# A linear layer with a low-rank update: all loads ahead of all stores, with transposed x kept on chip in bf16

## The chip, the cores and the metric

The kernel runs on one core of a Trainium2 chip. The metric is the device time of one execution in microseconds (us). The median of three runs of the kernel before is 165.0 us (164.87 to 165.51).

## The reference

`x` is 16 x 2048 rows of 256 numbers in float32, taken as 32,768 rows. `W` is 256 x 256, the low-rank part has rank 16.

```python
x_flat = x.reshape(-1, in_dim)
y = x_flat @ W
lora_out = x_flat @ lora_A
lora_out = lora_out * lora_E
lora_out = lora_out @ lora_B
y = y + scale * lora_out
```

The kernel folds the low-rank part into the weights once (`weff` = W + scale x A diag(E) B, in bf16) and then computes x times `weff`.

## The kernel before

Rows are spread over 128 partitions; a "row" below is one row of 256 numbers in each partition (128 KB over all partitions), so x has 256 such rows. `PLAN` cuts them into eight chunks of 16 to 48 rows. x arrives in float32 in the ring `xy` of 176 rows, and y is written over the same places, from which it is stored. So chunks 6 and 7 can be loaded only when stores have freed their places.

Per group of 16 rows (`G`), and in it per step of 8 rows (`S`):

- DVE casts 16 rows from `xy` to `xb` in bf16 (L199).
- PE transposes 8 rows at a time into PSUM (`ps_xt`, two buffers, L222); pairs of bf16 numbers travel as one float32, so a row takes one transpose of 128 columns.
- DVE copies the transposes of a step from PSUM into one of two buffers `xt` (L213).
- PE multiplies: for each half step of 4 rows (`Q`), 8 matmuls with `xt` as the loaded weights and `weff` moving, into one of two PSUM buffers `ps_y` (L230). Ahead of each half it waits for the buffer to be free (L227).
- ACT copies the half from `ps_y` into `xy` (L177); the last six halves are copied by DVE. The last copy of a chunk raises `s_rdy`, on which SP waits for the store; POOL hands the signal on to `s_y`, on which PE waits.

PE's work stands in one loop of 16 turns (L249), in which every address is fixed. The other engines' instructions are written out. All DMAs are issued by SP, in this order: W, chunk 0, the three small low-rank inputs, chunks 1 to 5, stores 0 to 2, loads 6 and 7, stores 3 to 7. So loads come first, then three stores, then two loads, then five stores. Three transfers are cut in two (`TAIL`), and stores 0 and 3 wait until the head of the load ahead of them has landed. `PAUSE` makes DVE wait ahead of chunk 4 until store 2 has landed.

Of the kernel before, what the change touches and what calls it, by code (L numbers as in the profile page):

```python
# [6 lines left out]

PLAN = [16, 32, 48, 48, 16, 16, 48, 32]  # L10

RING = 176

LEAD = 6
AFTER = {2: [6, 7]}


TAIL = 10
LOAD_TAILS, STORE_TAILS = (5, 7), (2,)

FIRST_STORES = {0: 5, 3: 7}

PAUSE = 4

G, S, Q = 16, 8, 4

LATE = 6


@with_exitstack  # L30
def kernel(
# [21 lines left out]
    CHUNKS = len(PLAN)  # L53
    assert K == M == KC * P and sum(PLAN) * P == N and all(b % G == 0 for b in PLAN)
# [24 lines left out]
    ps_aeb = ps_y[1][:, :KC, :]  # L79

    sem = tc.alloc_semaphore
    s_w, s_a, s_b, s_e = sem("s_w"), sem("s_a"), sem("s_b"), sem("s_e")
    s_in = [sem(f"s_in{i}") for i in range(CHUNKS)]
    s_head = {i: sem(f"s_head{i}") for i in LOAD_TAILS + STORE_TAILS}
    starts = [sum(PLAN[:i]) for i in range(CHUNKS)]
    places = [r % RING for r in starts]
    assert sum(PLAN[:LEAD]) <= RING and all(r + b <= RING for r, b in zip(places, PLAN))

    owners = {
        i: [j for j in range(LEAD) if places[j] < places[i] + PLAN[i] and places[i] < places[j] + PLAN[j]]  # L90
        for i in range(LEAD, CHUNKS)
    }

    again = max(j for js in owners.values() for j in js) + 1
    s_out = [sem(f"s_out{i}") for i in range(again + 1)]
# [5 lines left out]
    s_xt = sem("s_xt")  # L101
    s_p = sem("s_p")
    s_y = [sem(f"s_y{h}") for h in range(2)]
    s_rdy = sem("s_rdy")

    def rows_of(flat, i):
        b, r0 = PLAN[i], starts[i] * P
        return flat[r0:r0 + b * P, :].rearrange("(p b) k -> p b k", b=b)

    def ring_of(i):  # L110
        return xy[:, places[i]:places[i] + PLAN[i], :]


    def pieces(rows):
        return [(i, r) for i, b in enumerate(PLAN) for r in range(0, b, rows)]

    def rows_at(i, r, rows):
        return xy[:, places[i] + r:places[i] + r + rows, :]

    with tc.tile_critical(sync_engine=mybir.EngineType.SP, no_gpsimd_drain=True):  # L120
        sp, pe, dve, act, pool = nc.sync, nc.tensor, nc.vector, nc.scalar, nc.gpsimd


        def transfer(to, source, head, landed):
            cut = to.shape[1] - TAIL if head is not None else 0
            if cut:
                sp.dma_start(out=to[:, :cut, :], in_=source[:, :cut, :]).then_inc(head, 16)
            sp.dma_start(out=to[:, cut:, :], in_=source[:, cut:, :]).then_inc(landed, 16)
# [6 lines left out]
        sp.dma_start(out=a_sb[:], in_=lora_A.rearrange("(p c) r -> p c r", c=KC)).then_inc(s_a, 16)  # L135
        sp.dma_start(out=b_sb[:], in_=lora_B).then_inc(s_b, 16)
        sp.dma_start(out=e_sb[:], in_=lora_E[:, None]).then_inc(s_e, 16)
        for i in range(1, LEAD):
            load(i)
        for i in range(CHUNKS):  # L140
            sp.wait_ge(s_rdy, i + 1)
            if i in FIRST_STORES:
                sp.wait_ge(s_head[FIRST_STORES[i]], 16)
            transfer(
                rows_of(out_flat, i), ring_of(i), s_head[i] if i in STORE_TAILS else None, s_out[min(i, again)],
            )
            if i in AFTER:
                sp.wait_ge(s_head[i], 16)
                for later in AFTER[i]:
                    for j in owners[later]:  # L150

                        if j not in s_head or places[later] + PLAN[later] > places[j] + PLAN[j] - TAIL:
                            sp.wait_ge(s_out[j], 16)
                    load(later)
        for j in s_head:
            sp.wait_ge(s_head[j], 16)
        for i in range(len(s_out) - 1):
            sp.wait_ge(s_out[i], 16)


        pool.memset(ident[:], 0.0).then_inc(s_id, 1)  # L161
# [5 lines left out]
        pool.wait_ge(s_b, 16)  # L167
        pool.tensor_copy(out=b_bf[:], in_=b_sb[:]).then_inc(s_lora, 1)  # L168

        copies = pieces(Q)

        def y_of(q, engine, copy):
            i, r = copies[q]
            engine.wait_ge(s_p, q + 1)
            done = copy(out=rows_at(i, r, Q), in_=ps_y[q % 2][:])  # L177
            if r + Q == PLAN[i]:
                done.then_inc(s_rdy, 1)
            else:  # L180
                done.then_inc(s_y[q % 2], 1)

        for i in range(CHUNKS - 1):
            pool.wait_ge(s_rdy, i + 1).then_inc(s_y[((starts[i] + PLAN[i]) // Q - 1) % 2], 1)


        for q in range(len(copies) - LATE):
            y_of(q, act, act.copy)


        for g, (i, r) in enumerate(pieces(G)):
            if r == 0:
                if i in LOAD_TAILS:
                    dve.wait_ge(s_head[i], 16)
                dve.wait_ge(s_in[i], 16)
            if r == 0 and i == PAUSE:
                dve.wait_ge(s_out[again - 1], 16)

            dve.tensor_copy(out=xb[:], in_=rows_at(i, r, G)).then_inc(s_xb, 1)  # L199
            if g == 0:  # L200
                dve.wait_ge(s_e, 16)
# [8 lines left out]
            for k in range(g * G // S, (g + 1) * G // S):  # L210

                dve.wait_ge(s_t, k + 1)
                dve.tensor_copy(  # L213
                    out=xt[k % 2][:].rearrange("w j p c -> w j (p c)"), in_=ps_xt[k % 2][:].bitcast(BF16),
                ).then_inc(s_xt, 1)
        for q in range(len(copies) - LATE, len(copies)):
            y_of(q, dve, dve.tensor_copy)


        def transposes(k):  # L220
            for j in range(S):
                t = pe.transpose(ps_xt[k % 2][:, j, :], xb[:, k * S + j, :].bitcast(FP32), ident[:])  # L222
            t.then_inc(s_t, 1)

        def products(k):
            for h in range(S // Q):
                pe.wait_ge(s_y[h], 1).then_inc(s_y[h], -1)  # L227
                for j in range(Q):
                    for c in range(KC):
                        m = pe.matmul(  # L230
                            ps_y[h][:, j, :], xt[k % 2][:, h * Q + j, :, c], weff[:, c, :],
                            start=(c == 0), stop=(c == KC - 1),
                        )
                m.then_inc(s_p, 1)

        for h in range(2):
            pe.sem_inc(s_y[h], 1)
        pe.wait_ge(s_a, 16)
        pe.wait_ge(s_id, 2)
        for c in range(KC):  # L240
            t = pe.transpose(ps_at[:, c, :], a_sb[:, c, :], ident[:])  # L241
# [7 lines left out]
        with pe.Fori(0, sum(PLAN) // G):  # L249
            pe.wait_ge(s_xb, 1).then_inc(s_xb, -1)  # L250
            for k in range(G // S):
                transposes(k)
            for k in range(G // S):
                pe.wait_ge(s_xt, 1).then_inc(s_xt, -1)
                products(k)


    with tc.tile_critical(sync_engine=mybir.EngineType.SP, no_gpsimd_drain=True):
        nc.sync.wait_ge(s_out[again], 16 * (CHUNKS - again))


# [33 lines left out]
```

## Time and profile before

| what | value |
|---|---|
| median of three runs | 165.0 us |
| the profiled execution's own time | 165.08 us |
| its span, from first to last instruction | 163.3 us |
| bytes moved | 67.42 MB: 33.85 read, 33.55 written |
| DMA over the span | 413 GB/s |
| busy: PE, weight loads, DVE, ACT | 95.6, 78.5, 81.6, 57.2 us |

The profile is one execution. The page gives busy times of the engines, the span in 40 slices (each digit the busy share in tenths), the chain of work that ended last, and groups of instructions with count, mean duration and the idle time ahead of them with what ended it. The windows give the same numbers for chosen stretches, the timeline the instructions in order. PEld is the weight load of TensorE, which overlaps the matmuls; PEq and PEldq are its sequencer. DMA issues are listed with their size and the time to landing.

### The profile page before, as it was taken

The page shows a single profiled execution, that of the slowest core. Times are in us where ns is not written, and L with a number is a line of the kernel's source. Part 1 is how long each engine was busy: PE and PEld are TensorE (multiplying, and loading weights), DVE is VectorE, ACT ScalarE, POOL GpSimd, SP SyncE. Part 2 cuts the span into 40 slices and gives each one's busy share as a digit, 9 for nine tenths or more (in the row PEclk, how much of TensorE's full clock was granted, in tenths as well). Part 3 has the DMA queues.
Part 4 walks back from the last instruction along what each step waited for, and adds up shares of the span by engine and source line. Part 5 has one row for each costly group of instructions (what it writes and reads, how often), then busy time and mean ns, then how long its engine had stood idle before and what let it go on. Part 6 is the DMA issues. An engine that isn't in the chain of part 4 may idle for free. (4 is left out here: it accounts for less than half of the span.)

```text
span 163.3 us, 1919 instructions
## 1 busy us (share of the span) xinstructions
PE 95.6 (59%) x772; PEld 78.5 (48%) x772; DVE 81.6 (50%) x56; ACT 57.2 (35%) x59; POOL 2.8 (2%) x7
## 2 busy tenths in 40 slices
PE   0017989868978978985000898778989765400000
PEld 0006677746767757773000877657777563300000
DVE  0063767558486594750004385594774959700000
ACT  3000356482754845638000064735638400000000
POOL 1050000000000000000000000000000000000000
PEclk9999999999999999999755599999999999975555
DMA  5999998899889999998999898999997999999990
GB/s 157 417 421 482 498 409 385 385 554 409 385 381 403 430 446 458 417 501 372 419 408 450 385 494 354 436 414 486 470 457 327 429 437 449 494 421 403 441 409 16
DMA packets 3090, 67.42 MB, mean 413 GB/s; under 512 B 512, under 2 KB 528, under 8 KB 784
## 3 DMA queue, kind: packets, MB, share of 16 engines
q1 hardware_dynamic: 3088, 67.41, 96.9%
q14 instruction: 2, 0.02, 0.0%
HBM read 33.85 MB, written 33.55 MB: 413 GB/s over the span
## 5 line engine op out<-in xcount | busy, mean ns | idle before, releaser
L177 ACT COPY xy<-ps_y 128x1024 f32<-128x1024 f32 x58 | 55.9, 1016 | 72.4 <-PE ps_y L230 72.4
L230 PE MATMUL ps_y<-weff,xt 128*128 128x256 bf16 x512 | 62.6, 273 | 17.0 <-PEq L227 16.8
L230 PEld LDWEIGHTS ps_y<-weff,xt 128*128 128x128 bf16 x512 | 47.0, 98 | 32.0 <-issue 24.9
L213 DVE COPY xt<-ps_xt 128x2048 bf16<-128x2048 bf16 x32 | 37.9, 1219 | 31.2 <-PE ps_xt L222 31.2
L199 DVE CAST xb<-xy 128x4096 bf16<-128x4096 f32 x16 | 36.6, 2286 | 28.4 <-DMA out_dram<-xy 15.1
L222 PE MATMUL ps_xt<-ident,xb 128*128 128x128 f32 x256 | 34.0, 291 | 16.8 <-PEq L250 16.8
L222 PEld LDWEIGHTS ps_xt<-ident,xb 128*128 128x128 f32 x256 | 31.3, 151 | 18.1 <-issue 18.0
L177 DVE COPY xy<-ps_y 128x1024 f32<-128x1024 f32 x6 | 7.1, 1217 | 0.2
L241 PE MATMUL ps_y<-ident,a_sb 128*16 128x128 f32 x2 | 0.6, 399 | 9.6 <-DMA a_sb<-in_lora_A_dram 9.6
L241 PEld LDWEIGHTS ps_y<-ident,a_sb 128*16 128x16 f32 x2 | 0.1, 94 | 9.6 <-DMA a_sb<-in_lora_A_dram 9.6
L168 POOL CAST b_bf<-b_sb 16x256 bf16<-16x256 f32 x1 | 2.1, 2122 | 8.1 <-DMA b_sb<-in_lora_B_dram 8.1
L245 PE MATMUL ps_y<-b_bf,ate 16*128 16x256 bf16 x2 | 0.6, 403 | 1.9 <-DVE ate L203 1.9
L177 ACT ACT_TABLE_LOAD x1 | 1.3, 1283 | 0.9 <-SPq L120 0.9
L245 PEld LDWEIGHTS ps_y<-b_bf,ate 16*128 16x128 bf16 x2 | 0.1, 105 | 2.4 <-DVE ate L203 2.4
L209 DVE TENSOR_TENSOR weff<-w_sb,ps_y 128x512 bf16<-128x512 f32 x1 | 0.7, 689 | 0.8 <-PE ps_y L245 0.8
L203 DVE TENSOR_SCALAR ate<-ps_y,e_sb 16x256 bf16<-16x256 f32 x1 | 0.5, 466 | 0.0
L163 POOL TENSOR_SCALAR_AFFINE_SELECT ident<-ident 128x128 f32<-128x128 f32 x1 | 0.3, 293 | 0.2 <-POOL ident L161 0.2
L161 POOL MEMSET ident<- 128x128 f32 x1 | 0.2, 205 | 0.5 <-SPq L120 0.5
L276 POOL MEMSET const-float32-0.0<- 128x1 f32 x1 | 0.1, 98 | 0.2 <-issue 0.2
L276 POOL MEMSET const-bfloat16-1.0<- 128x1 bf16 x1 | 0.1, 101 | 0.0
L276 POOL MEMSET const-uint8-127<- 128x1 uint8 x1 | 0.1, 101 | 0.0
L276 POOL MEMSET const-float32-1.0<- 128x1 f32 x1 | 0.1, 98 | 0.0
## 6 DMA issues: line engine op xcount, KB each, us to landing
xy<-in_x_dram SPq DMA_DIRECT2D x3, 6144.0 KB, 30.1
out_dram<-xy SPq DMA_DIRECT2D x2, 6144.0 KB, 22.1
out_dram<-xy SPq DMA_DIRECT2D x2, 4096.0 KB, 18.6
out_dram<-xy SPq DMA_DIRECT2D x3, 2048.0 KB, 22.8
out_dram<-xy SPq DMA_DIRECT2D x1, 4864.0 KB, 27.3
xy<-in_x_dram SPq DMA_DIRECT2D x2, 2048.0 KB, 28.2
xy<-in_x_dram SPq DMA_DIRECT2D x1, 4096.0 KB, 16.0
xy<-in_x_dram SPq DMA_DIRECT2D x1, 2816.0 KB, 24.3
```

Of the source, the lines that this page charges most:

```text
L163: pool.affine_select(out=ident[:], in_=ident[:], compare_op=mybir.AluOpType.not_equal, fill=1.0, base=0, pattern=[[-1, P]], channel_multip ...
L168: pool.tensor_copy(out=b_bf[:], in_=b_sb[:]).then_inc(s_lora, 1)
L177: done = copy(out=rows_at(i, r, Q), in_=ps_y[q % 2][:])
L199: dve.tensor_copy(out=xb[:], in_=rows_at(i, r, G)).then_inc(s_xb, 1)
L203: dve.tensor_scalar(out=ate[:], in0=ps_at, scalar1=e_sb[:], scalar2=float(scale), op0=mybir.AluOpType.mult, op1=mybir.AluOpType.mult,).the ...
L209: dve.tensor_add(out=weff[:], in0=w_sb[:], in1=ps_aeb).then_inc(s_lora, 1)
L213: dve.tensor_copy(out=xt[k % 2][:].rearrange("w j p c -> w j (p c)"), in_=ps_xt[k % 2][:].bitcast(BF16),).then_inc(s_xt, 1)
L222: t = pe.transpose(ps_xt[k % 2][:, j, :], xb[:, k * S + j, :].bitcast(FP32), ident[:])
L230: m = pe.matmul(ps_y[h][:, j, :], xt[k % 2][:, h * Q + j, :, c], weff[:, c, :], start=(c == 0), stop=(c == KC - 1),)
L241: t = pe.transpose(ps_at[:, c, :], a_sb[:, c, :], ident[:])
L245: m = pe.matmul(ps_aeb[:, c, :], ate[:, c, :], b_bf[:], start=True, stop=True)
L276: nc = _bacc.Bacc("TRN2", target_bir_lowering=False, num_devices=1)
```

## The change

The order of all transfers changes to W, chunk 0, the small inputs, all other loads, then all stores. There are eleven chunks, ten of three steps (24 rows) and one of two (16 rows). Four float32 buffers hold them, three of 24 rows and one of 16. Chunk i is loaded into buffer `X_AT[i]`, which is free when the chunk before it there has been transposed (`s_t`); y of chunk i is collected in buffer `Y_AT[i]`, which is free when the store before it there has landed (`s_io` at 32).

What carries x from the load stage to the store stage is `xt`, now with room for 26 of the 32 steps. PE runs the transposes of the first 24 steps in a loop of their own. A second loop alternates one step of products with one step of transposes, eight times; then PE waits for the last copies, and a third loop runs the remaining 24 steps of products, one step a turn. In the second and third loop the step's place in `xt` comes from the loop's variable (`bass.ds(slot, 1)`).

DVE casts 8 rows at a time into two buffers `xb`. Of the copies of transposes, ACT takes every third of the first 24, DVE the others. Of the copies of y, ACT takes all up to half step 15 and two of three after that, DVE the others. The chunk's end is now signalled per half (`s_rdy[h]`), and POOL hands on both.

```diff
-PLAN = [16, 32, 48, 48, 16, 16, 48, 32]
-RING = 176
-LEAD = 6
-AFTER = {2: [6, 7]}
-TAIL = 10
-LOAD_TAILS, STORE_TAILS = (5, 7), (2,)
-FIRST_STORES = {0: 5, 3: 7}
-PAUSE = 4
-G, S, Q = 16, 8, 4
-LATE = 6
+S, Q = 8, 4
+PLAN = [3] * 10 + [2]
+BUFFERS = [3, 3, 3, 2]
+X_AT = [0, 1, 2, 0, 1, 2, 0, 1, 2, 0, 3]
+Y_AT = [1, 2, 0, 1, 2, 0, 1, 2, 0, 1, 3]
+KEPT, FIRST = 26, 18
+AHEAD, MIXED = 24, 8
+def acts_transposes(k):
+    return k % 3 == 2 and k < AHEAD
+def vectors_y(q):
+    return q >= 16 and q % 3 == 1
...
-    xy = sbuf("xy", [P, RING, K], FP32)
-    xb = sbuf("xb", [P, G, K], BF16)
-    xt = [sbuf(f"xt{s}", [P, S, P, KC], BF16) for s in range(2)]
+    xy = sbuf("xy", [P, sum(BUFFERS) * S, K], FP32)
+    xb = [sbuf(f"xb{s}", [P, S, K], BF16) for s in range(2)]
+    xt = sbuf("xt", [P, KEPT, S, P, KC], BF16)
...
+    def place(k):
+        return (k + FIRST) % KEPT
...
         def load(i):
-            transfer(ring_of(i), rows_of(x_flat, i), s_head[i] if i in LOAD_TAILS else None, s_in[i])
+            if x_before[i] is not None:
+                sp.wait_ge(s_t, first[x_before[i]] + PLAN[x_before[i]])
+            sp.dma_start(out=rows_at(X_AT[i], 0, PLAN[i] * S), in_=rows_of(x_flat, i)).then_inc(s_io[i], 16)
...
-        for i in range(1, LEAD):
+        for i in range(1, CHUNKS):
             load(i)
         for i in range(CHUNKS):
...
+            for h in range(H):
+                sp.wait_ge(s_rdy[h], i + 1)
+            sp.dma_start(out=rows_of(out_flat, i), in_=rows_at(Y_AT[i], 0, PLAN[i] * S)).then_inc(s_io[i], 16)
...
+        for i in range(CHUNKS - 1):
+            for h in range(H):
+                pool.wait_ge(s_rdy[h], i + 1).then_inc(s_y[h], 1)
...
         def y_of(q, engine, copy):
+            k, h = q // H, q % H
+            i = chunk[k]
+            if y_before[i] is not None and known.get(engine) != i:
+                engine.wait_ge(s_io[y_before[i]], 32)
+            known[engine] = i
             engine.wait_ge(s_p, q + 1)
...
+        def copy_transposes(k, engine, copy):
+            engine.wait_ge(s_t, k + 1)
+            if k >= KEPT:
+                engine.wait_ge(s_p, (k - KEPT + 1) * H)
+            copy(
+                out=xt[:, place(k)].rearrange("w j p c -> w j (p c)"), in_=ps_xt[k % 2][:].bitcast(BF16),
+            ).then_inc(s_c[k % 2], 1)
...
+        for k in range(STEPS):
+            if k != first[chunk[k]]:
+                if k - 2 >= first[chunk[k]]:
+                    vectors_transposes(k - 2)
             else:
+                for j in range(max(0, k - 2), k):
+                    vectors_transposes(j)
+            round_step(k)
...
+        def transposes(b):
+            pe.wait_ge(s_xb, 1).then_inc(s_xb, -1)
+            pe.wait_ge(s_c[b], 1).then_inc(s_c[b], -1)
             for j in range(S):
-                t = pe.transpose(ps_xt[k % 2][:, j, :], xb[:, k * S + j, :].bitcast(FP32), ident[:])
+                t = pe.transpose(ps_xt[b][:, j, :], xb[b][:, j, :].bitcast(FP32), ident[:])
             t.then_inc(s_t, 1)

-        def products(k):
-            for h in range(S // Q):
+        def products(slot):
+            step = xt[:, bass.ds(slot, 1)]
+            for h in range(H):
                 pe.wait_ge(s_y[h], 1).then_inc(s_y[h], -1)
                 for j in range(Q):
                     for c in range(KC):
                         m = pe.matmul(
-                            ps_y[h][:, j, :], xt[k % 2][:, h * Q + j, :, c], weff[:, c, :],
-                            start=(c == 0), stop=(c == KC - 1),
+                            ps_y[h][:, j, :], step[:, :, h * Q + j, :, c].rearrange("w s p -> w (s p)"),
+                            weff[:, c, :], start=(c == 0), stop=(c == KC - 1),
                         )
                 m.then_inc(s_p, 1)
...
+        with pe.Fori(0, AHEAD // 2):
+            for b in range(2):
+                transposes(b)
         pe.wait_ge(s_lora, 3)
-        with pe.Fori(0, sum(PLAN) // G):
-            pe.wait_ge(s_xb, 1).then_inc(s_xb, -1)
-            for k in range(G // S):
-                transposes(k)
-            for k in range(G // S):
-                pe.wait_ge(s_xt, 1).then_inc(s_xt, -1)
-                products(k)
+        with pe.Fori(place(0), place(0) + MIXED - 1, 2) as slot:
+            for b in range(2):
+                products(slot + b)
+                transposes(b)
+        for b in range(2):
+            pe.wait_ge(s_c[b], 1)
+        with pe.Fori(place(MIXED), place(MIXED) + STEPS - MIXED) as slot:
+            products(slot)
```

More of the change, by code (lines that the diff above doesn't have):

```diff
@@ L52 @@
     KC = K // P
-    CHUNKS = len(PLAN)
-    assert K == M == KC * P and sum(PLAN) * P == N and all(b % G == 0 for b in PLAN)
+    H = S // Q
+    CHUNKS, STEPS = len(PLAN), sum(PLAN)
+    assert K == M == KC * P and STEPS * S * P == N
     def sbuf(name, shape, dt):
@@ L81 @@
     sem = tc.alloc_semaphore
[L82 to L95, printed above, removed]
+    s_w = sem("s_w")
+    s_l = sem("s_l")
+    s_io = [sem(f"s_io{i}") for i in range(CHUNKS)]
     s_id = sem("s_id")
@@ L100 @@
     s_t = sem("s_t")
-    s_xt = sem("s_xt")
+    s_c = [sem(f"s_c{h}") for h in range(2)]
     s_p = sem("s_p")
-    s_y = [sem(f"s_y{h}") for h in range(2)]
-    s_rdy = sem("s_rdy")
-    def rows_of(flat, i):
[L107 to L115, printed above, removed]
@@ L117, in rows_at @@
-    def rows_at(i, r, rows):
-        return xy[:, places[i] + r:places[i] + r + rows, :]
+    s_y = [sem(f"s_y{h}") for h in range(H)]
+    s_rdy = [sem(f"s_rdy{h}") for h in range(H)]
+    first = [sum(PLAN[:i]) for i in range(CHUNKS)]
+    chunk = [i for i, b in enumerate(PLAN) for _ in range(b)]
+    at = [sum(BUFFERS[:b]) for b in range(len(BUFFERS))]
+    assert all(b <= BUFFERS[X_AT[i]] and b <= BUFFERS[Y_AT[i]] for i, b in enumerate(PLAN))
+    x_before = [max((j for j in range(i) if X_AT[j] == X_AT[i]), default=None) for i in range(CHUNKS)]
@@ L120, with rows_at @@
+    y_before = [max((j for j in range(i) if Y_AT[j] == Y_AT[i]), default=None) for i in range(CHUNKS)]
+    def rows_of(flat, i):
+        r0, n = first[i] * S * P, PLAN[i] * S
+        return flat[r0:r0 + n * P, :].rearrange("(p b) k -> p b k", b=n)
+    def rows_at(buffer, r, rows):
+        return xy[:, at[buffer] * S + r:at[buffer] * S + r + rows, :]
+    def place(k):
+        return (k + FIRST) % KEPT
     with tc.tile_critical(sync_engine=mybir.EngineType.SP, no_gpsimd_drain=True):
         sp, pe, dve, act, pool = nc.sync, nc.tensor, nc.vector, nc.scalar, nc.gpsimd
[L124 to L128, printed above, removed]
@@ L130, in load @@
         def load(i):
-            transfer(ring_of(i), rows_of(x_flat, i), s_head[i] if i in LOAD_TAILS else None, s_in[i])
+            if x_before[i] is not None:
+                sp.wait_ge(s_t, first[x_before[i]] + PLAN[x_before[i]])
+            sp.dma_start(out=rows_at(X_AT[i], 0, PLAN[i] * S), in_=rows_of(x_flat, i)).then_inc(s_io[i], 16)
         sp.dma_start(out=w_sb[:], in_=W.rearrange("(p c) m -> p c m", c=KC)).then_inc(s_w, 16)
         load(0)
-        sp.dma_start(out=a_sb[:], in_=lora_A.rearrange("(p c) r -> p c r", c=KC)).then_inc(s_a, 16)
@@ L136 @@
-        sp.dma_start(out=b_sb[:], in_=lora_B).then_inc(s_b, 16)
-        sp.dma_start(out=e_sb[:], in_=lora_E[:, None]).then_inc(s_e, 16)
-        for i in range(1, LEAD):
+        sp.dma_start(out=a_sb[:], in_=lora_A.rearrange("(p c) r -> p c r", c=KC)).then_inc(s_l, 16)
+        sp.dma_start(out=b_sb[:], in_=lora_B).then_inc(s_l, 16)
+        sp.dma_start(out=e_sb[:], in_=lora_E[:, None]).then_inc(s_l, 16)
+        for i in range(1, CHUNKS):
             load(i)
         for i in range(CHUNKS):
[L141 to L158, printed above, removed]
+            for h in range(H):
+                sp.wait_ge(s_rdy[h], i + 1)
+            sp.dma_start(out=rows_of(out_flat, i), in_=rows_at(Y_AT[i], 0, PLAN[i] * S)).then_inc(s_io[i], 16)
+        for i in range(CHUNKS - 3):
+            sp.wait_ge(s_io[i], 32)
         pool.memset(ident[:], 0.0).then_inc(s_id, 1)
@@ L166 @@
         ).then_inc(s_id, 1)
-        pool.wait_ge(s_b, 16)
+        pool.wait_ge(s_l, 48)
         pool.tensor_copy(out=b_bf[:], in_=b_sb[:]).then_inc(s_lora, 1)
-        copies = pieces(Q)
+        for i in range(CHUNKS - 1):
+            for h in range(H):
+                pool.wait_ge(s_rdy[h], i + 1).then_inc(s_y[h], 1)
+        known = {}
         def y_of(q, engine, copy):
-            i, r = copies[q]
-            engine.wait_ge(s_p, q + 1)
-            done = copy(out=rows_at(i, r, Q), in_=ps_y[q % 2][:])
-            if r + Q == PLAN[i]:
-                done.then_inc(s_rdy, 1)
-            else:
-                done.then_inc(s_y[q % 2], 1)
@@ L183 @@
[L183 to L201, printed above, removed]
+            k, h = q // H, q % H
@@ new lines, in y_of @@
+            i = chunk[k]
+            if y_before[i] is not None and known.get(engine) != i:
+                engine.wait_ge(s_io[y_before[i]], 32)
+            known[engine] = i
+            engine.wait_ge(s_p, q + 1)
+            done = copy(out=rows_at(Y_AT[i], (k - first[i]) * S + h * Q, Q), in_=ps_y[h][:])
+            last = k == first[i] + PLAN[i] - 1
+            done.then_inc(s_rdy[h] if last else s_y[h], 1)
+        def copy_transposes(k, engine, copy):
[5 more added lines that the diff above has]
+            ).then_inc(s_c[k % 2], 1)
@@ new lines, with round_step @@
+        for k in range(STEPS):
+            if acts_transposes(k):
+                assert k < AHEAD
+                copy_transposes(k, act, act.copy)
+        for q in range(STEPS * H):
+            if not vectors_y(q):
+                y_of(q, act, act.copy)
+        def round_step(k):
+            i = chunk[k]
+            if k == first[i]:
+                dve.wait_ge(s_io[i], 16)
+            if k >= 2 and acts_transposes(k - 2):
+                dve.wait_ge(s_t, k - 1)
+            dve.tensor_copy(
+                out=xb[k % 2][:], in_=rows_at(X_AT[i], (k - first[i]) * S, S),
+            ).then_inc(s_xb, 1)
@@ L202, with vectors_transposes @@
+        def vectors_transposes(k):
+            if not acts_transposes(k):
+                copy_transposes(k, dve, dve.tensor_copy)
+        for k in range(STEPS):
+            if k != first[chunk[k]]:
+                if k - 2 >= first[chunk[k]]:
+                    vectors_transposes(k - 2)
+            else:
+                for j in range(max(0, k - 2), k):
+                    vectors_transposes(j)
+            round_step(k)
+            if k == 0:
+                dve.wait_ge(s_l, 48)
                 dve.wait_ge(s_lpe, 1)
@@ L209 @@
                 dve.tensor_add(out=weff[:], in0=w_sb[:], in1=ps_aeb).then_inc(s_lora, 1)
[L210 to L220, printed above, removed]
+        for j in range(STEPS - 2, STEPS):
+            vectors_transposes(j)
+        for q in range(STEPS * H):
+            if vectors_y(q):
+                y_of(q, dve, dve.tensor_copy)
+        def transposes(b):
+            pe.wait_ge(s_xb, 1).then_inc(s_xb, -1)
+            pe.wait_ge(s_c[b], 1).then_inc(s_c[b], -1)
             for j in range(S):
-                t = pe.transpose(ps_xt[k % 2][:, j, :], xb[:, k * S + j, :].bitcast(FP32), ident[:])
+                t = pe.transpose(ps_xt[b][:, j, :], xb[b][:, j, :].bitcast(FP32), ident[:])
             t.then_inc(s_t, 1)
-        def products(k):
-            for h in range(S // Q):
+        def products(slot):
+            step = xt[:, bass.ds(slot, 1)]
+            for h in range(H):
                 pe.wait_ge(s_y[h], 1).then_inc(s_y[h], -1)
@@ L230, in products @@
                         m = pe.matmul(
-                            ps_y[h][:, j, :], xt[k % 2][:, h * Q + j, :, c], weff[:, c, :],
-                            start=(c == 0), stop=(c == KC - 1),
+                            ps_y[h][:, j, :], step[:, :, h * Q + j, :, c].rearrange("w s p -> w (s p)"),
+                            weff[:, c, :], start=(c == 0), stop=(c == KC - 1),
                         )
                 m.then_inc(s_p, 1)
-        for h in range(2):
+        for h in range(H):
             pe.sem_inc(s_y[h], 1)
-        pe.wait_ge(s_a, 16)
+        for b in range(2):
+            pe.sem_inc(s_c[b], 1)
+        pe.wait_ge(s_l, 48)
         pe.wait_ge(s_id, 2)
@@ L246 @@
         m.then_inc(s_lpe, 1)
+        with pe.Fori(0, AHEAD // 2):
+            for b in range(2):
+                transposes(b)
         pe.wait_ge(s_lora, 3)
-        with pe.Fori(0, sum(PLAN) // G):
-            pe.wait_ge(s_xb, 1).then_inc(s_xb, -1)
-            for k in range(G // S):
-                transposes(k)
-            for k in range(G // S):
-                pe.wait_ge(s_xt, 1).then_inc(s_xt, -1)
-                products(k)
+        with pe.Fori(place(0), place(0) + MIXED - 1, 2) as slot:
+            for b in range(2):
+                products(slot + b)
+                transposes(b)
+        for b in range(2):
+            pe.wait_ge(s_c[b], 1)
+        with pe.Fori(place(MIXED), place(MIXED) + STEPS - MIXED) as slot:
+            products(slot)
     with tc.tile_critical(sync_engine=mybir.EngineType.SP, no_gpsimd_drain=True):
-        nc.sync.wait_ge(s_out[again], 16 * (CHUNKS - again))
+        for i in range(CHUNKS - 3, CHUNKS):
+            nc.sync.wait_ge(s_io[i], 32)
 _INS = ['x', 'W', 'lora_A', 'lora_B', 'lora_E', 'scale']
```

## The prediction

> **What bounds the kernel now.** First the page: how full each engine and the transfers are.
>
> ```profile
> span 163.3 us, 1919 instructions
> PE 95.6 (59%) x772; PEld 78.5 (48%) x772; DVE 81.6 (50%) x56; ACT 57.2 (35%) x59; POOL 2.8 (2%) x7
> ...
> DMA  5999998899889999998999898999997999999990
> ...
> q1 hardware_dynamic: 3088, 67.41, 96.9%
> ```
>
> No compute engine passes 59%, while the one DMA queue is busy in every slice but the ends. The chain of waits that ended last holds only the last products and copies, because a DMA runs behind them; so I went on to the windows, to see what a stage of pure loads or pure stores moves.
>
> ```profile
> 60.00:84.00 24.00, 13.80 (x118) 11.16 (x116) 8.69 (x6) 11.38 (x12) 0.00 (x0) 0.92 1.00 429
> 88.00:108.00 20.00, 15.16 (x115) 12.89 (x116) 13.23 (x9) 7.72 (x8) 0.00 (x0) 0.86 0.97 417
> 112.00:140.00 28.00, 21.70 (x186) 17.82 (x184) 20.84 (x16) 10.61 (x12) 0.00 (x0) 1.00 1.00 431
> 140.00:158.00 18.00, 0.89 (x8) 0.55 (x6) 2.15 (x2) 0.00 (x0) 0.00 (x0) 0.63 0.98 422
> ```
>
> Last column GB/s, the one before it the share of the DMA engines: stores (60 to 84, 112 to 158) move 422 to 431, a load stage with its turn 417. The loads are better read in the timeline, where the first cast of a chunk waits for its landing.
>
> ```profile
> 19.31 2.29 DVE L199 CAST xb<-xy 128x4096 bf16<-128x4096 f32 x1 [0.64 <-DMA xy<-in_x_dram]
> ...
> 24.47 1.91 PE L230 MATMUL ps_y<-weff,xt 128*128 128x256 bf16 x16 [0.69 <-PEq L227]
> 25.54 1.93 ACT L177 COPY xy<-ps_y 128x1024 f32<-128x1024 f32 x2 [2.45 <-PE ps_y L230]
> 26.70 1.94 PE L230 MATMUL ps_y<-weff,xt 128*128 128x256 bf16 x16 [0.33 <-PEq L227]
> ...
> 33.85 2.29 DVE L199 CAST xb<-xy 128x4096 bf16<-128x4096 f32 x1 [1.94 <-DMA xy<-in_x_dram]
> ```
>
> Chunk 2 (48 rows a partition) lands 14.54 us after chunk 1: 0.303 us a row. The middle lines give a product step of 8 rows: 2.23 us from start to start. In it, half a step's 8 matmuls at a pitch of 0.109 us take 0.87; the other 1.36 are the tail of the last matmul, ACT's copy and the hops.
>
> ```profile
> L177 ACT COPY xy<-ps_y 128x1024 f32<-128x1024 f32 x58 | 55.9, 1016 | 72.4 <-PE ps_y L230 72.4
> L213 DVE COPY xt<-ps_xt 128x2048 bf16<-128x2048 bf16 x32 | 37.9, 1219 | 31.2 <-PE ps_xt L222 31.2
> L177 DVE COPY xy<-ps_y 128x1024 f32<-128x1024 f32 x6 | 7.1, 1217 | 0.2
> w_sb<-in_W_dram SPq DMA_DIRECT2D x1, 256.0 KB, 2.7
> L249 PEldq ALU_OP  x16: 36/36/42, 21.0 to 139.9; - x16
> ```
>
> These are the prices used below; the last row, of the loop line, is the only register arithmetic that PE does now.
>
> **The bytes.** They stay the same, and so does the start (W, then chunk 0). Chunk 0 grows from 16 to 24 rows and lands at 9.35 + 8 x 0.303 = 11.8; each further chunk takes 24 x 0.305 = 7.32 (0.303 with a little for each DMA), so chunk 8 lands at 70.4, chunk 9 at 77.7 and chunk 10 (16 rows) at 82.5. All 33.55 MB of stores at 427 GB/s (between the windows' 422 and 431) take 78.6, or 7.37 a chunk. Unbroken, the last store lands at 161.1. Before, it landed at 142.18 + 19.8 = 162.0 (its issue, and its time to landing), and the span ended 1.3 later; the execution was 165.08 for a span of 163.3, so 1.8 lies outside, and the median of the runs is 165.0. Fed without a break the new kernel gives 161.1 + 1.3 + 1.8 = 164.2. The gain of 0.9 is the two turns that go: the load of 48 rows behind the stores took 14.8 (87.8 to 102.67, the casts that waited for the last store and for that load) against 14.54, the store of 48 rows behind the loads 15.1 (from issues and times to landing: 85.57 + 26.9 = 112.5 to 109.42 + 18.1 = 127.5).
>
> **Load stage.** Per chunk DVE does three casts of 8 rows (half of 2.286 us, taken as 1.17) and two copies of 1.22, 5.9 of 7.32. PE does 3 x 8 transposes at 0.109, 2.6. ACT takes every third copy, unseen so far with this form; twice its 1.016 row, 2.0, hidden since it has no y yet. Loads 3 to 9 wait on SP until a chunk's transposes are done, and the stores queue behind them there; but two chunks, 14.6 us, are then still in the queue, and the work needs some 7. Cost nothing; cold transposes (16 in 3.55 us at 90.3) would add 2.6 a chunk to PE, still inside. POOL's relays and SP's three more issues at 0.33 to 0.43 are as well covered.
>
> The granted clock rows of the windows are 0.50 for 90.2 to 93.6, where PE did transposes alone, and 0.98 for 93.6 to 94.2: transposes by themselves raise the clock. [...]
>
> **The mixed stretch** is where I put the loss. From transposes 24 on, one step of products alternates with one of transposes, and the first three stores hang on it. Chunk 8 at 70.4: cast 71.6, transposes 24 end at 72.6, products 1 at 74.4, transposes 25 at 75.3, products 2 at 77.0, transposes 26 at 77.9; ACT's copy ends at 78.2 and store 0 is issued with loads still in the queue. At a chunk's edge DVE copies transposes 26 (79.3) before it casts step 27 (80.4), while PE has only products 3 to do: transposes 27 end at 81.4, products 4 at 83.1, transposes 28 at 84.0, products 5 at 85.8; store 1 issued at 87.0, due (first data) at 82.5 + 7.4. The same edge again: transposes 29 at 86.6, copy 88.0, cast 89.2, transposes 30 at 90.2, products 7 at 91.9, transposes 31 at 92.8, copy 94.1. Ahead of the last loop PE waits for that copy, and products 8, queued behind the wait, end at 95.9, y of chunk 2 at 97.2. Store 1 lands at 82.5 + 14.7 = 97.2, and a queue that ran dry needs the 2.7 us of the W row less 0.6 of data, 2.1, to flow again: a gap of 2.2 even at an unchanged pitch.
>
> **The address arithmetic** is what the trace does not show: each of the 512 product weight loads takes its address from a register. Lower bound nothing: 36 ns of ALU_OP fit under the pitch of 109. A gain has no source, as array time doesn't fall. Upper bounds: from that ALU_OP to the sequencer's next instruction are 97 ns, from one L227 wait to the next 151 with 16 PE instructions between them, so a PE instruction costs it at most 9. One operation a matmul is then 97 + 18 = 0.116 us, one as dear as a wait 0.160, two operations 0.212. I take 0.116, the row of the same kind of instruction. Six products lie on the mixed path: 6 x 16 x 0.007 = 0.7, so the gap is 2.9. In the loop of products alone, a step becomes 8 x 0.116 + 1.36 = 2.29 on ACT, and 0.20 more where DVE copies, one in three: 2.36, or 7.1 a chunk against 7.37 of store. No further gap; the cover is thin, and ends at a pitch of about 0.128.
>
> [...]
>
> **Sum:** 161.1 + 2.9 = 164.0 last landing, + 1.3 = 165.3 span, + 1.8 = 167.1 us.
>
> **Rivals.** *PE's sequencer becomes the bound.* At 0.160 both halves of a step queue on it: 2 x (8 x 0.160 + 0.15) = 2.86 against 2.46 of store. 23 steps behind the mixed stretch add 23 x 0.4 = 9, the mixed stretch some 2 more than forecast: 178. At 0.212, 3.69 a step: about 198. For it: nothing can run ahead of the waits for a free PSUM half. Against it: 36 ns.
>
> *Faster, because nothing but the turns matters.* Place: the edges at 87.8 and 112.4, plus 11 long stores at the 433 GB/s that the loads show: 82.5 + 256 x 0.303 = 160.1, so 163.2 us. It decides if store 2 is issued before 95.1, that is if the mixed chain is 2.9 shorter than worked out (casts and copies overlapping better at the two chunk edges). *Half of that:* gap and gain cancel, 164.2 to 165.8. That the loads do not come first after all, because SP stands before load 3 to 9, needs 7 us more per chunk than the rows give; I leave it out.
>
> **How the numbers follow.** Forecast (a gap of 1.5 to 4 at store 2, pitch to 0.12: 165.8 to 168.5) 0.45; sequencer-bound 0.23 (169 to 198); cancelled 0.17; faster 0.15 (162.5 to 164.2). About 0.5%, 0.8 us, is what a measurement can tell from no change, so faster 0.15, same 0.17, slower 0.68. The range leaves out the quicker half of the faster case and the sequencer case above its 0.160 price: 163.6 to 178. The forecast's own range is 165.8 to 168.5.
>
> **What would show it.** In the changed profile: a dip of the DMA row near 97 to 100 and none later; SP's longest wait in the store stage for the y of chunk 2; products at a pitch of 0.109 to 0.12 with one ALU_OP or fewer per matmul; product steps 2.3 to 2.4 apart; no gap at 82. Wrong if the DMA row dips in every chunk (sequencer bound), if GB/s is full through 97 (no gap), or if the rate itself changes in long pure stretches.

## The result, and the profile after

The new kernel takes 178.03 us (177.71 to 178.36, four runs) against 164.99 us (164.87 to 165.51, four runs): 1.078 times the time before (95% interval 1.075 to 1.082). The prediction said slower, 167.1 us; the loss is 13 us, where 2.1 were forecast. The profiled execution took 178.34 us for a span of 176.6, so 1.7 lies outside.

The page of the new kernel, the same rows as before:

```profile
span 176.6 us, 2587 instructions
PE 120.8 (68%) x772; PEld 90.7 (51%) x772; DVE 86.5 (49%) x74; ACT 64.3 (36%) x57; POOL 1.6 (1%) x7
...
DMA  6999999999999999999949269888896988896995
...
q1 hardware_dynamic: 3520, 67.41, 89.7%
q8 instruction: 1, 0.02, 0.0%
```

Read the DMA row, 4.4 us a digit. The first 20 slices, the loads and most of store 0, have no break. Then come two dips (4 from 88 us, 2 and 6 from 97), and after that hardly two nines in a row: 8s and 6s in every chunk. The prediction expected one dip and named a dip in every chunk as the mark of the sequencer-bound rival. No engine passes 68%, and yet the queue is only 89.7% full: so something sets the pace that the busy times do not show. The windows give the stages:

```profile
60.00:82.00 22.00, 19.26 (x123) 15.92 (x122) 15.68 (x15) 10.13 (x9) 0.00 (x0) 0.71 1.01 432
82.00:104.00 22.00, 18.56 (x139) 14.16 (x137) 12.86 (x11) 11.03 (x12) 0.00 (x0) 0.92 0.68 287
104.00:160.00 56.00, 46.61 (x320) 30.80 (x318) 16.61 (x14) 26.64 (x27) 0.00 (x0) 1.00 0.89 379
```

As before, the last two columns are DMA share and GB/s: 432 in the loads, 287 in the mixed stretch, 379 in the loop of products alone. Both later stages lose. Store by store, from the issues and landings in the trace:

```
store        0      1      2       3       4 to 7            8       9       10
issued    80.66  90.35  102.48  110.90  119.35 to 144.67  153.12  161.56  167.18
landed    89.59  99.11  111.29  119.70  128.15 to 153.47  162.44  170.29  175.14
after the
landing before  7.31   9.52   12.18   8.41    8.43 to 8.45     8.97    7.85    4.85
```

Store 0 follows the last load (82.28) without a gap. Stores 1 and 2 come late, and from store 3 on each chunk takes 8.44 us where the prediction has 7.37. SP waits for y, hardly for a DMA (the queue's own waits):

```profile
SPq L139 <- ACT xy L169: 98.7, 11, 16.1
```

What holds the y? Three lines of the timeline, the loop of products at full clock:

```profile
104.60 2.37 PE L243 MATMUL ps_y<-weff,xt 128*128 128x256 bf16 x16 [0.43 <-PEq L240]
...
105.85 2.17 ACT L169 COPY xy<-ps_y 128x1024 f32<-128x1024 f32 x2 [1.53 <-PE ps_y L243]
...
107.42 2.35 PE L243 MATMUL ps_y<-weff,xt 128*128 128x256 bf16 x16 [0.45 <-PEq L240]
```

A step is 2.82 us from start to start; it was 2.23 before. Its 16 matmuls run 2.37 us as one block, where a block took 1.91 to 1.95 before. In the groups, the copies of y cost what they did, with long idle time ahead of them, put down to the matmuls:

```profile
L169 ACT COPY xy<-ps_y 128x1024 f32<-128x1024 f32 x48 | 48.2, 1014 | 46.1 <-PE ps_y L243 44.8
L169 DVE COPY xy<-ps_y 128x1024 f32<-128x1024 f32 x16 | 19.6, 1224 | 47.2 <-PE ps_y L243 47.2
```

Idle time ahead of the copies alone does not say what sets the step, because ACT waited for the matmuls in the kernel before too (72.4 us). The rows of the matmuls' own line show what is new on PE's sequencer (PEldq; durations in ns, smallest, median, largest):

```profile
L243 PEldq FUSED_REGOPS  x512: 46/46/60, 69.6 to 165.7; - x171
L243 PEld LDWEIGHTS ps_y<-weff,xt x512: 96/97/152, 70.5 to 165.8; 128*128 x171
L243 PE MATMUL ps_y<-weff,xt x512: 272/282/421, 70.7 to 165.8; 128*128 128x256 bf16 x171
```

One register operation stands ahead of each of the 512 product weight loads. Its 46 ns are not its price. In the trace it starts at 107.448, its weight load at 107.543, the next register operation at 107.572: a pitch of 0.124 us, bound by the sequencer. The loop's line has the rest:

```profile
L273 PEldq MOVE  x25: 29/37/37, 97.9 to 163.4; - x25
L273 PEldq ALU_OP  x24: 36/36/36, 100.5 to 165.8; - x24
L273 PEldq COMPARE_BRANCH  x24: 76/208/218, 100.6 to 165.9; - x24
```

In one turn the trace has the ALU_OP at 106.710, COMPARE_BRANCH at 106.807, MOVE at 107.073, the PSUM wait at 107.168 and the first register operation at 107.319. The turn costs 0.46 us up to the wait, and a wait that is already satisfied 0.151. A step on the sequencer is 16 x 0.124 + 2 x 0.151 + 0.46 + about 0.05 = 2.80; from its third step on, the steps of this loop are 2.81 apart on average. Nor does the sequencer stand still there: from 105.5 us on each wait comes 29 to 95 ns behind the instruction ahead of it, so the buffer was always free already.

### The profile page after: what moved, and what is told of

Same layout as the page of the kernel before. It is cut to its first block, busy times and chain, and to the rows that moved or that the text cites. A ratio compares the mean times of both kernels' runs of the same rounds, so it can differ in the third digit from the quotient of the medians.

```text
span 176.6 us, 2587 instructions
## 1 busy us (share of the span) xinstructions
PE 120.8 (68%) x772; PEld 90.7 (51%) x772; DVE 86.5 (49%) x74; ACT 64.3 (36%) x57; POOL 1.6 (1%) x7
## 3 DMA queue, kind: packets, MB, share of 16 engines
q1 hardware_dynamic: 3520, 67.41, 89.7%
## 5 line engine op out<-in xcount | busy, mean ns | idle before, releaser
L243 PE MATMUL ps_y<-weff,xt 128*128 128x256 bf16 x512 | 74.8, 287 | 12.2 <-PEq L240 12.0
L243 PEld LDWEIGHTS ps_y<-weff,xt 128*128 x512 | 50.8, 99 | 35.2 <-issue 22.0
L169 ACT COPY xy<-ps_y 128x1024 f32<-128x1024 f32 x48 | 48.2, 1014 | 46.1 <-PE ps_y L243 44.8
L234 PE MATMUL ps_xt<-ident,xb 128*128 128x128 f32 x256 | 46.7, 350 | 20.4 <-PEq L232 20.3
L234 PEld LDWEIGHTS ps_xt<-ident,xb 128*128 128x128 f32 x256 | 39.9, 184 | 26.7 <-issue 26.6
L197 DVE CAST xb<-xy 128x2048 bf16<-128x2048 f32 x32 | 38.2, 1221 | 14.6 <-DMA xy<-in_x_dram 14.6
L169 DVE COPY xy<-ps_y 128x1024 f32<-128x1024 f32 x16 | 19.6, 1224 | 47.2 <-PE ps_y L243 47.2
L177 DVE COPY xt<-ps_xt 128x2048 bf16<-128x2048 bf16 x24 | 29.3, 1223 | 15.4 <-PE ps_xt L234 15.4
L177 ACT COPY xt<-ps_xt 128x2048 bf16<-128x2048 bf16 x8 | 14.9, 1866 | 55.7 <-PE ps_xt L234 55.7
L256 PE MATMUL ps_y<-ident,a_sb 128*16 128x128 f32 x2 | 0.6, 401 | 12.1 <-DMA e_sb<-in_lora_E_dram 12.1
L256 PEld LDWEIGHTS ps_y<-ident,a_sb 128*16 128x16 f32 x2 | 0.1, 90 | 12.1 <-DMA e_sb<-in_lora_E_dram 12.1
L152 POOL CAST b_bf<-b_sb 16x256 bf16<-16x256 f32 x1 | 0.9, 879 | 10.4 <-DMA e_sb<-in_lora_E_dram 10.4
```

What stands on the lines that cost most here:

```text
L169: done = copy(out=rows_at(Y_AT[i], (k - first[i]) * S + h * Q, Q), in_=ps_y[h][:])
L177: copy(out=xt[:, place(k)].rearrange("w j p c -> w j (p c)"), in_=ps_xt[k % 2][:].bitcast(BF16),).then_inc(s_c[k % 2], 1)
L197: dve.tensor_copy(out=xb[k % 2][:], in_=rows_at(X_AT[i], (k - first[i]) * S, S),).then_inc(s_xb, 1)
L234: t = pe.transpose(ps_xt[b][:, j, :], xb[b][:, j, :].bitcast(FP32), ident[:])
L243: m = pe.matmul(ps_y[h][:, j, :], step[:, :, h * Q + j, :, c].rearrange("w s p -> w (s p)"), weff[:, c, :], start=(c == 0), stop=(c == KC ...
```

## The experiments

Theory A: PE's sequencer sets the step (16 register operations, two waits, one loop turn, one after the other). Theory B: the ring of three y buffers sets 8.44 us a chunk. Later theories are named where they come up. Times are medians, of two executions for fixed_last, fixed_mixed, turns_of_4, same_slot and half_registers and of four for the others; ratios are against the kernel before on the same chip.

| run | us (range) | ratio (interval) |
|---|---|---|
| fixed_all | 179.59 (178.31 to 180.55) | 1.092 (1.086 to 1.098) |
| fixed_last | 179.31 (179.01 to 179.61) | 1.088 (1.085 to 1.092) |
| fixed_mixed | 175.26 (175.19 to 175.34) | 1.064 (1.061 to 1.066) |
| turns_of_4 | 175.39 (174.83 to 175.96) | 1.065 (1.060 to 1.069) |
| same_slot | 168.90 (168.29 to 169.50) | 1.025 (1.021 to 1.030) |
| half_registers | 169.92 (169.43 to 170.41) | 1.032 (1.027 to 1.036) |
| staged | 171.42 (169.83 to 172.44) | 1.038 (1.032 to 1.043) |
| same_slot_no_wait | 167.25 (166.55 to 168.51) | 1.014 (1.011 to 1.017) |
| staged_small | 176.36 (174.82 to 176.82) | 1.072 (1.069 to 1.074) |

**Written out, with fixed addresses.** fixed_all writes both product loops out; fixed_last only the last, fixed_mixed only the mixed one.

```diff
-        with pe.Fori(place(0), place(0) + MIXED - 1, 2) as slot:
-            for b in range(2):
-                products(slot + b)
-                transposes(b)
+        for k in range(MIXED):
+            products(place(k))
+            transposes(k % 2)
...
-        with pe.Fori(place(MIXED), place(MIXED) + STEPS - MIXED) as slot:
-            products(slot)
+        for k in range(MIXED, STEPS):
+            products(place(k))
```

> Products written out with fixed addresses in both product stages; the loop of transposes stays. Theory A (PE's sequencer is the bound: a step of products costs it 16 register operations at a pitch of 0.124, two waits of 0.151 and a loop turn of 0.46, 2.81 us in a row): no FUSED_REGOPS left, products at 0.109, a store every 7.3 us instead of 8.44, stores 1 on time, store 2 late by about 2.2; last landing 160.3 + 2.2 = 162.5, time about 165.7. Theory B (the ring of three y buffers sets the 8.44, a chunk waits for the store three before it): stores stay 8.44 apart, time about 178.

> Only the last 24 steps of products have fixed addresses; the mixed loop keeps its registers. Theory A: store 1 stays late by 2.2, store 2 by about 4 (its last step is cheaper now), and from store 3 on every landing is 7.3 behind the one before: the 7.8 us of lateness of stores 3 to 10 go; time about 169.7. Theory B: about 178.

> Only the eight mixed steps have fixed addresses; the last loop keeps its registers. Theory A: store 1 on time, store 2 late by about 3, then every store late by 1.13 as before: time about 174. Theory B: the mixed stretch is not what counts, about 178.

The first two missed by 10 to 14 us. The steps did fall to 2.23 to 2.49 us, as A says, and in fixed_last stores 3 to 5 each landed 7.1 to 7.25 after the one before, which B excludes. But single steps of 7.09, 4.16 and 7.72 us (fixed_all) and of 9.03 and 7.01 (fixed_last) gave it all back. The page of fixed_all has four code transfers, and holes in the DMA row:

```profile
DMA  6999999999999999999996698829999889943995
...
q8 instruction: 4, 0.07, 0.1%
```

Its timeline at the second hole:

```profile
110.38 1.22 DVE L169 COPY xy<-ps_y 128x1024 f32<-128x1024 f32 x1 [2.33 <-PE ps_y L243]
...
115.99 4.79 PE L243 MATMUL ps_y<-weff,xt 128*128 128x256 bf16 x27 [4.87 <-issue]
```

PE stands 4.87 us and waits for nothing that the profile shows ("issue"). The transfer of 16 KB of code starts at 113.53 in this hole; those at 133.87 and 157.20 lie in or beside the other two long steps, and the one at 89.09 goes with no long step. Each takes about 1 us on one DMA engine. In all five holes of fixed_all and fixed_last PE starts again 1.3 to 1.6 us after a code transfer has ended, which is what one would see if PE stood for the code. Behind the hole the granted clock is 0.5 (115.6 to 119.0), so the next step is slow as well (27 matmuls in 4.79). What the transfer itself waited for, the trace does not show, only when it ran. PE stood 4.87 us in this hole, 5.59 in the longest of fixed_all and 6.79 in the longest of fixed_last.

fixed_mixed has two code transfers (88.60, 97.14) and keeps the register loop for the last 24 steps: 175.26, near the expected 174. Its store 1 is issued at 87.67, 2.7 earlier than in the new kernel, and from store 2 on the stores are again 8.4 to 8.6 apart. So the mixed stretch is worth about 3 us, and the last loop is the larger part. Not all of the 3 is the addresses: in the profiled executions the granted clock rose at 68.35 us here and at 72.56 in the new kernel, and so the mixed stretch began earlier here.

**Fewer loop turns.**

```diff
-        with pe.Fori(place(MIXED), place(MIXED) + STEPS - MIXED) as slot:
-            products(slot)
+        with pe.Fori(place(MIXED), place(MIXED) + STEPS - MIXED - 3, 4) as slot:
+            for b in range(4):
+                products(slot + b)
```

> The last loop does four steps in a turn instead of one, with the register addresses kept: the price of a loop turn by itself. Theory A: a step costs 2.81 - 3/4 x 0.46 = 2.47, a chunk 7.41 against 7.31 of store; of the 7.8 us of stores 3 to 10 some 1 stays; time about 171. If the register operations alone set the step, the time hardly moves from 178.

The direction of A, but smaller: 2.6 us off the new kernel's time where about 7 were expected, steps of 2.5 to 2.98 and chunks of 7.9 to 8.4. With the turn gone from three steps in four, the sequencer needs 16 x 0.124 + 0.35 = 2.33 there; I had counted the turn alone. The measured steps lie above that, because the copy chain sets them here, and it is longer than the prediction's formula has it. When PE's sequencer has waited for a free buffer, the first weight load comes 0.25 us or more later if a register operation stands ahead of it (wait 111.242, FUSED_REGOPS 111.393, load 111.502), and 0.076 later with a fixed address (same_slot: wait 116.445, load 116.521). That puts some 0.17 more into the chain: 8 x 0.124 + 1.36 + 0.17 = 2.52, and 0.26 more where DVE copies (same_slot's 2.49 against 2.23), 2.78. The steps without a loop turn measure 2.50 to 2.61 and 2.77 to 2.82; those with one 2.77 to 2.98.

**The loops, with no address to compute.** The addresses are fixed: two places in the mixed loop, one in the last.

```diff
-                products(slot + b)
+                products(place(MIXED) + b)
...
-            products(slot)
+            products(place(MIXED))
```

> Both product loops stay loops, but every turn reads the same place of xt at a fixed address (so y is that of other rows): the register operations alone are taken away, and no long code comes in their place. Theory A: no FUSED_REGOPS; a step of the last loop falls from 2.81 to 2.23 where ACT copies and 2.49 where DVE copies one half, under the 2.44 of a store; store 2 late by some 2, nothing after it; time 165.6 to 166.5. Theory B (ring of y buffers): stores 8.4 apart, about 178. Theory C (written-out code was slow because of something in the store stage other than code loading): stalls of 4 to 6 us here too, about 176.

This is the deciding run: 9.1 us of the 13.0 go. Loops, buffers, waits and order are all as in the new kernel (the loop's MOVE goes with the address: once instead of 25 times); B would have left them. Part of the 9.1, about 1.3 by the profiled executions, can be the clock, which rose at 68.82 us here. The matmuls' line has no register operation, and the page one hole:

```profile
L243 PEld LDWEIGHTS ps_y<-weff,xt x512: 96/98/98, 69.9 to 151.1; 128*128 128x128 bf16 x171
L243 PE MATMUL ps_y<-weff,xt x512: 269/272/273, 70.0 to 151.2; 128*128 128x256 bf16 x171
```

```profile
DMA  6999999998999999999999929999989899999991
```

Steps are 2.23 to 2.49, store 1 lands without a gap (7.38), and store 2 2.98 late, at the place that the prediction named. It missed its range by 2.4 us for two reasons that I had left out: that gap is larger than I had allowed, and stores 3 to 8 land 7.54 to 7.63 apart although they are issued every 7.0.

**Half the register operations.** Only one of the two weight loads of a row computes its address.

```diff
+            other = xt[:, place(MIXED):place(MIXED) + 1]
...
-                            ps_y[h][:, j, :], step[:, :, h * Q + j, :, c].rearrange("w s p -> w (s p)"),
+                            ps_y[h][:, j, :], (step, other)[c][:, :, h * Q + j, :, c].rearrange("w s p -> w (s p)"),
```

> Of the two matmuls that make a product one keeps its register address, the other reads a fixed place (so y is partly that of other rows): 8 register operations a step instead of 16. Theory A, a chain on the sequencer that counts only where it is the longest: 8 x 0.124 + 2 x 0.151 + 0.46 = 1.75 a step, under the 2.3 of the copies, so the whole loss of the last loop goes and the time is 166 to 167.5. If each register operation costs its share wherever it stands, half the loss stays: about 172.

169.92 lies between the two, and 1.0 above same_slot: half of the operations cost a ninth of the 9.1 us. The sequencer is not the bound here: the fixed instructions cost it little, so a step takes it some 8 x 0.124 + 0.81 plus at most 16 x 0.009, under 2.0 us. But the operations are not free below that bound. Steps are 2.38 to 2.65 where same_slot has 2.23 to 2.49, and the copy chain's 0.17 behind each wait accounts for it (wait 117.038, FUSED_REGOPS 117.189, load 117.284). The time hardly shows it because the stores are then issued every 7.5 us, and in same_slot they land every 7.6 although they are issued every 7.0.

**The wait at the end of the mixed stretch.** In same_slot and in the new kernel PE waits, ahead of its last loop, for the copies of the last transposes. Here it does so behind the loop, and ACT, not DVE, copies the first half of step 8 (the lines below are against same_slot).

```diff
-    return q >= 16 and q % 3 == 1
+    return q >= 18 and q % 3 == 1
...
-        for b in range(2):
-            pe.wait_ge(s_c[b], 1)
         with pe.Fori(place(MIXED), place(MIXED) + STEPS - MIXED) as slot:
             products(place(MIXED))
+        for b in range(2):
+            pe.wait_ge(s_c[b], 1)
```

> As same_slot (every turn of both product loops reads one fixed place, so y is of the wrong rows), and in addition PE does not wait for the copies of the last two transposes ahead of its last loop (it takes that wait behind the loop; the fixed place is one that those copies do not write), and ACT, not DVE, copies the first half of step 8. In same_slot store 2 was issued at 98.57 us and its queue had run dry: it landed 2.98 us late, and step 8 came 4.47 us after step 7. Theory (the second term of the loss is this wait at the end of the mixed stretch, not something in the queue): step 8 comes about 3.2 us after step 7, store 2 is issued some 1.3 us earlier, at about 97.2, lands about 1.6 us late, and the time falls by about 1.3 from 168.9 to 167.6. Rival (the queue needs this pause anyway, or the late engine sets the end): store 2 moves but the last landing does not, 168.5 to 169.

The timeline of same_slot, then of this run:

```profile
92.90 1.04 PE L234 MATMUL ps_xt<-ident,xb 128*128 128x128 f32 x8
95.55 1.91 PE L243 MATMUL ps_y<-weff,xt 128*128 128x256 bf16 x16 [1.61 <-PEq L240]
```

```profile
94.56 1.04 PE L234 MATMUL ps_xt<-ident,xb 128*128 128x128 f32 x8
95.44 1.91 PE L243 MATMUL ps_y<-weff,xt 128*128 128x256 bf16 x16
```

From the last transposes to step 8, 2.65 us become 0.88, and the median time falls to 167.25, the expected 167.6 within its spread. Store 2 is not issued earlier (98.51), against what I wrote: in this execution the clock stayed at 0.5 until 73.26 (68.82 in same_slot), the mixed stretch began over a microsecond later, and store 1 took the delay instead (8.26). Two executions with different clocks can't be laid over each other; the medians and the step itself can.

**The reference's computation without register addresses.** DVE copies each kept step into a fixed slot, from which PE reads; ACT copies all of y. staged has two slots, 24 kept steps, and the last two transposes behind step 9; staged_small has one slot of two halves and less code.

```diff
+    xw = [sbuf(f"xw{s}", [P, S, P, KC], BF16) for s in range(2)]
...
+            dve.tensor_copy(
+                out=xw[k % 2][:].rearrange("w j p c -> w (j p c)"),
+                in_=xt[:, place(k)].rearrange("w j p c -> w (j p c)"),
+            ).then_inc(s_xw, 1)
...
-        def products(slot):
-            step = xt[:, bass.ds(slot, 1)]
+        def products(b):
+            pe.wait_ge(s_xw, 1).then_inc(s_xw, -1)
```

> A version meant to be faster than both: DVE, idle in the store stage, copies each kept step into one of two places with fixed addresses, and PE's loops read those, as in the kernel before; ACT copies all y; transposes 30 and 31 come after products 9, so store 2 no longer waits for them. Keeps 24 steps instead of 26. Theory A: step 2.23 as in the kernel before, all stores back to back but for at most 1 at store 1 or 2; last landing 160.5 to 162, time 163.5 to 165.2. If the copies to the fixed places take 1.2 us each they lengthen the mixed stretch and store 1 or 2 is late by 1 to 2: up to 167. Theory B: about 178.

> The computation is the reference's. As staged (DVE copies each kept step to a fixed slot, PE's addresses are fixed), but there is one slot of two halves, filled half by half, so that one loop body of one step serves all products, and the last loop needs no wait for the copies of the last transposes. PE's code is about 220 instructions where staged had about 359. Theory (the 4.3 us at store 3 of staged were the fetch of code ahead of its last loop; PE's code that stays under a block needs none): no code transfer in the store stage, store 3 issued before the queue runs dry, steps about 2.5 us apart in the last loop, stores 7.3 to 7.7 us apart; stores 1 and 2 late by 1 to 2 us each, as DVE now casts, copies and stages (3.1 us a step) in the mixed stretch; 167 to 169. Rival (the staging copies themselves made the stall, or the loop turn's 0.46 us with two waits a half adds up on PE): a gap at store 3 remains or steps of 2.7 and more, 171 to 174.

Both missed. staged lost 1.56 and 1.2 us at stores 1 and 2 and 4.3 at store 3. Its executions scatter by 1.5%, and the profiled one is the slowest, so only its large gaps are read. When staged_small was planned, the 4.3 us were put down to a code transfer in staged (106.96), but that one came after the stall:

```profile
100.18 2.35 DVE L177 COPY xt<-ps_xt 128x2048 bf16<-128x2048 bf16 x2 [2.42 <-PE ps_xt L256]
102.45 1.28 DVE L210 COPY xw<-xt 128x2048 bf16<-128x2048 bf16 x2
...
103.43 4.34 PE L265 MATMUL ps_y<-weff,xw 128*128 128x256 bf16 x24 [2.42 <-PEq L262]
```

Step 10 starts at 103.43, as soon as its staging is done, and DVE had put that staging behind the copies of the last two transposes. Then the granted clock is 0.5 until 106.65, so the step is slow too. So staged_small, which also has another order on DVE, tested a cause that was not there. It has no code transfer in the store stage (that code under a block needs none, as its theory assumes, no run shows by itself), and its last loop is as fast as staged's (2.23 to 2.28),

```profile
106.30 1.95 PE L261 MATMUL ps_y<-weff,xw 128*128 128x256 bf16 x16 [0.34 <-PEq L258]
...
108.52 1.95 PE L261 MATMUL ps_y<-weff,xw 128*128 128x256 bf16 x16 [0.28 <-PEq L258]
```

at 2.23 to 2.29 us a step, and stores issued every 6.8. But with one slot DVE's casts, copies and stagings queue up in the mixed stretch: PE waits 3.03 us for the staging ahead of steps 3 and 6, the granted clock falls to 0.5 there for 3.4 us each time, and the steps grow to 5.8 us; stores 1 and 2 land 10.94 and 12.82 after the store before. I had priced DVE's sum (3.1 a step) and not its order. No run reached the time before.

## Why the prediction failed

**The load stage** came as worked out: chunks 8, 9 and 10 land at 70.09, 77.39 and 82.28 (70.4, 77.7 and 82.5 forecast), 7.30 to 7.31 a chunk, no gap at 82. This part of the sum stands.

**The step that failed is the loop of products alone.** "a step becomes 8 x 0.116 + 1.36 = 2.29 on ACT ... 2.36": the pitch was nearly right, 0.124 for 0.116 (and under the 0.160 and 0.212 of the dearer prices), but the step measured 2.81. Two terms were missing. First, the copy chain has some 0.17 more behind each wait, as turns_of_4 and half_registers show. At a pitch of 0.124 it takes 2.52 on ACT and, with DVE's copies, about 2.62 on average (same_slot's 2.33 and 0.29 more): 7.9 a chunk, already over the store's 7.37. Second, the copy chain was taken for the only chain. The two waits and the loop turn were left at nothing because before they lay beside array time: the sequencer ran far ahead (16 PE instructions within 151 ns) and did its bookkeeping while the array worked. With a register operation ahead of every weight load it does not get ahead in this loop: from step 10 on every matmul starts 0.10 us behind its register operation, and 0.30 + 0.46 us of bookkeeping stand in series. That makes 2.80, which passes the copy chain and sets the step. The cover was named, and its end put at a pitch of 0.128; by these two sums it was gone at 0.124. From store 2 to the last landing this makes 63.9 us where 56.5 were forecast: 7.4 of the 11.1 us by which the last landing (175.14) missed.

**The rival had the mechanism and, by chance, the time.** "PE's sequencer becomes the bound" gave 178 by a price of 0.160 a matmul and a step of 2.86; the step is 2.81, from 0.124 a matmul and a turn that the rival did not count. It had 0.23. What spoke against it, 36 ns of ALU_OP, was a busy time; the row's 97 ns to the next instruction stood beside it.

**The mixed stretch** had the right place and the wrong size. The gap at store 2 was forecast with 2.9 us; store 1 came 1.9 us later than forecast and store 2 another 1.9. SP issued store 1 at 90.35, not 87.0. By the runs: same_slot issues it at 87.86, so the chain as priced without addresses was 0.9 short. The start costs about 1.3: step 2 begins at 77.17 against 75.67 in same_slot, and at 77.34 in same_slot_no_wait, which has no register operation but the same late clock (and loads that land 0.4 later). The rest, some 1.2, is the addresses. The wait for the copies ahead of the last loop is in the forecast; same_slot_no_wait prices it at 1.7 us, together with the copy that it moves from DVE to ACT. From store 1's issue to store 2's the new kernel takes 12.1 us and same_slot 10.7; about 0.7 of the difference, an estimate, is a second cold stretch, granted clock 0.5 from 99.86 to 103.27, in which step 8's block takes 3.08 us (2.35 later on).

**The clock.** The prediction held that transposes raise it. In the new kernel, where PE does nothing but transposes from 14 to 70 us, it is granted 1.0 from 17.94 to 28.18, then changes about every 3.4 us, and stays at 0.5 from 48.66 to 72.56. So it rose four times while PE did transposes alone (at 17.94, 31.60, 38.42 and 45.25), but did not stay up; the prediction's sentence was too simple. From 72.56 us on the transposes of the mixed stretch ran at full clock (1.04 to 1.07 us for eight, where eight at 69.00 took 1.94). The cold start cost about 1.3 us.

**The drained queue.** 2.1 us for a dry queue to flow again was too much: a store of 3,072 KB issued into an empty queue lands after 8.8 us, 7.3 of them data at the pace of the loads (7.30 to 7.31 a chunk), so 1.5.

**The forecast of a fed queue.** 164.2 for unbroken feeding was not reached by any run. same_slot_no_wait comes nearest. Its profiled execution, 168.51 us, still has 0.9 and 1.6 us of gaps at stores 1 and 2, so fully fed it would take about 166.0, an estimate and no better than the time before. What then remains over 164.2 is mostly the stores that land every 7.5 to 7.6 us. No run shows a gain from the order.

## What to carry to other kernels

Price an address computed at run time by the pitch from instruction to instruction on the sequencer (here 0.124 us, for an operation of 46 ns), and then add up everything that the sequencer does in a turn: two waits and a loop turn, 0.30 + 0.46 us a step here, cost nothing while it ran ahead of the array and stood in series once it did not. Look also at what stands between a wait and the first weight load behind it: the register operation there put some 0.17 us into the chain through each wait of half_registers, although the sequencer had time. Writing the loop out was no free way out here: with the last loop written out, PE stood up to 6.79 us, and each of the five holes ended 1.3 to 1.6 us after a block of code had come in among the stores. And ask what a new order can win if all goes well; here the sum of the bytes left 0.8 us, against a change that touched every instruction of the bounding chain.

## What the hardware showed beyond that

- **Register addresses:** in the new kernel one FUSED_REGOPS of 46 ns ahead of each weight load, a pitch of 0.124 us from one to the next, 0.25 us from a wait to the first weight load (0.076 with a fixed address in same_slot), and 0.46 us for a loop turn with COMPARE_BRANCH at 208 ns.
- **One of the 16 completions of a store lags in long stretches of stores.** In same_slot the time between the first and the last of the 16 completions of a store grows from 0.25 us at store 2 to 1.87 at store 8 (0.54, 0.83, 1.13, 1.35, 1.65 between), and it is one completion that comes late: the other 15 lie within 0.2. In the loads it stays at 0.64. So it grows by 0.22 to 0.30 us a store, and stores issued every 7.0 us land every 7.54 to 7.63, about that much over the 7.30 to 7.31 of a chunk of loads in the new kernel. In the kernel before it reaches 2.31 at the last store; in the new kernel, whose queue runs dry in every chunk, it is near 0.3 (0.81 once).
- **Code blocks** of 16 KB during bulk stores: PE stood up to 6.79 us (fixed_last) and started again 1.3 to 1.6 us after the transfer had ended, and the half clock behind the hole added to it.
